# Expert weights two rows to a partition, gathers spread over two groups, results added later as a one-hot times two split parts

## The chip, the cores and the metric

The kernel runs on one core of a Trainium2 chip. The core has five engines that run side by side: TensorE (PE, matrix products; its weight loads are listed apart as PEld), VectorE (DVE), ScalarE (ACT), GpSimd (POOL) and SyncE (SP, which here only issues transfers). Sixteen DMA engines move data between the main memory and the core's on-chip memory. The metric is the time of one execution on the device, in microseconds (us); lower is better.

## The reference, cut to what matters

The program is four transformer layers on 256 tokens of width 1024, all in float32: two layers of a first block (each a mixer and a mixture of experts) and two dense layers of a second block. The change touches the mixture of experts:

```python
def expert_choice_ffn(h, w_router, w1, w3, w2):
    n_tok, d = h.shape[1], h.shape[2]
    cap = EC_FACTOR * n_tok // N_EXPERTS                  # 2 * 256 // 16 = 32
    aff = jax.nn.softmax(jnp.einsum('bnd,de->bne', h, w_router).astype(jnp.float32), axis=-1)
    gate, idx = lax.top_k(jnp.swapaxes(aff, 1, 2), cap)
    xs = jax.vmap(lambda hb, ib: hb[ib])(h, idx)
    a = jnp.einsum('becd,edf->becf', xs, w1)
    b = jnp.einsum('becd,edf->becf', xs, w3)
    y = jnp.einsum('becf,efd->becd', jax.nn.silu(a) * b, w2) * gate[..., None].astype(h.dtype)

    def combine(yb, ib):
        return jnp.zeros((n_tok, d), h.dtype).at[ib.reshape(-1)].add(yb.reshape(-1, d))
    return jax.vmap(combine)(y, idx)
```

Each of 16 experts picks 32 tokens, runs them through three 1024 x 1024 matrices (4 MB each) and the results are added back to the tokens with the gate as factor. In layer 0 this is done for two streams (256 latent and 256 context tokens) with the same weights, in layer 1 for the latent stream alone. So each layer reads 16 x 3 x 4 MB = 192 MB of expert weights, once.

## The kernel before, in words

`build` runs `even_mixer(0)`, `moe(0)`, `odd_mixer(1)`, `moe(1)` and `layers2`. All weights come through `wload`, which takes the next slot (a buffer of 128 partitions x 2048 float32, 1 MB) and issues one transfer on SP's queue. A slot can be filled again only when its last reader on PE is done, and SP issues in program order, so a slot that is still in use holds up all loads behind it. The slots come from `self.plan` while that list lasts, and then from `self.slots` in turn. In `moe(0)` `self.slots` has 13 entries; the plan adds two buffers that are needed later for scatter tables (`early`) and three that are needed later for gathered tokens (`spare`: the tiles xs3, xs2, xs1), so the first 18 loads find a buffer each, and from then on 13 are cycled. In `moe(1)` there are 16 slots, and 21 in the first pass.

`moe` makes the router's softmax and a top-32 of each expert, and from it one-hot matrices: `OH` (token x slot, for gathering) and `og` (the same with the gate as value). Experts run in four groups of four. `gather(g, ...)` multiplies the tokens (stationary operand, 128 columns at a time) by a group's columns of `OH`, which gives the tokens of four experts transposed (tile gps), and applies gain and shift on its way to `xs[g]`. `expert(e, ...)` takes each matrix in four loads of two row blocks (rows k*128 to k*128+127, so that partition p gets row p of each block: two runs of 4 KB); tokens are the stationary operand, the weights stream past. The hidden vector is transposed (hps) and multiplied by the third matrix (py), and the rows go to `y4` with the factor m5. After the first expert `scatter_rows` transposes `og` (tiles t, om) and broadcasts m5 (rb). `combine(g, ...)` multiplies the transposed `og` by the group's `y4` in float32 (tile cmb) and adds the product to the tokens.

In program order: gather of group 0 inside expert 0; gathers of groups 1, 2 and 3 behind experts 1, 2 and 3; a combine behind each of experts 3, 7, 11 and 15. The tile framework may start an instruction earlier on its engine where the operands are ready. The last combine carries hooks that start the next stage (`odd_start` or `block2_start`).

For comparison with other transfers: the modulation weights (`modulation`, in_mod_w) are also loaded by `wload`, with kk = 1 and n = 2048, that is one run of 8 KB per partition.

Of the kernel before, what the change touches and what calls it, by code (L numbers as in the profile page):

```python
# [80 lines left out]
class Net:  # L81
# [70 lines left out]

    def wload(self, src, kk, n):
        slot = self.plan.pop(0) if self.plan else None
        if slot is None:
            slot = self.slots[self.turn % len(self.slots)]
            self.turn += 1
        if type(slot) is tuple:
            pool, tag, bufs = slot
            t = pool.tile([P, 2048], F32, tag=tag, name="w", bufs=bufs)  # L160
        else:
            t = slot
        v = t[:, :kk * n].rearrange("p (k n) -> p k n", k=kk)
        self.nc.sync.dma_start(out=v, in_=src.rearrange("(k p) n -> p k n", p=P))
        return v
# [826 lines left out]
    def moe(self, L, streams):  # L992
        nc, A = self.nc, self.A
        ns = len(streams)
        T = 32 * ns
        HF = 128 // T
        CW = D // HF
        from contextlib import ExitStack
        with ExitStack() as st:
# [4 lines left out]
            n = self.extra[L]  # L1004
# [3 lines left out]
            act, wk = self.act, self.wk  # L1008
            ga = self.gain("norm2_g", L, 4)
            b3 = self.mod_cols(L, 3)  # L1010
            base = self.slots
# [14 lines left out]
            ps = self.tp.tile([P, 256], F32, tag="t", name="affT")  # L1026
# [47 lines left out]

            def room(i):
                return act.tile([P, 2048], F32, tag="om%d" % i, name="om%d" % i)
            early = [room(i) for i in range(ns)]

            def xs_tile(g):
                n = NK * 4 * T if g == 0 else 2048  # L1080
                xs = (rb[-1] if L == 0 and g > 1 else act).tile([P, n], F32, tag="xs%d" % g, name="xs%d" % g, bufs=1)
                return xs[:, :NK * 4 * T].rearrange("p (k e j) -> p k e j", k=NK, e=4)
# [21 lines left out]
            def expert(e, xs, y4, hooks={}):  # L1104
                pa = ab.tile([P, CW], F32, tag="ab", name="pa")
                pb = ab.tile([P, CW], F32, tag="ab", name="pb")
                for dst, nm in ((pa, "exp_w1"), (pb, "exp_w3")):
                    for k0 in range(0, NK, 2):
                        if (nm, k0) in hooks:
                            hooks[nm, k0]()  # L1110
                        w = self.wload(A[nm][L, e, k0 * P:(k0 + 2) * P, :], 2, D)
                        for kk in range(2):
                            for h in range(HF):
                                nc.tensor.matmul(dst[h * T:(h + 1) * T, :], xs[:, k0 + kk, e % 4, :],  # L1114
                                                 w[:, kk, h * CW:(h + 1) * CW], start=k0 + kk == 0,
                                                 stop=k0 + kk == NK - 1, skip_group_check=True)
# [5 lines left out]
                for j in range(nj):  # L1122
                    nc.tensor.transpose(ps[:, j, :], h[:, j * P:(j + 1) * P], self.ident)
                hT = wk.tile([P, 4, P], F32, tag="ht", name="ht")
                self.evac(hT[:, :nj, :], ps[:, :nj, :])
                py = yp.tile([P, CW], F32, tag="md", name="py")
                for k0 in range(0, NK, 2):
                    w = self.wload(A["exp_w2"][L, e, k0 * P:(k0 + 2) * P, :], 2, D)
                    for kk in range(2):
# [8 lines left out]
                if r == 0:  # L1138
                    y4 += [wk.tile([P, D], F32, tag="y4_%d" % s, name="y4") for s in range(ns)]
                for s in range(ns):  # L1140
# [4 lines left out]

            def combine(g, y4, hooks={}):
                i = 0
                for s, x in enumerate(streams):
                    for t in range(2):
                        for n in range(2):  # L1150
                            ps = self.mm.tile([P, 512], F32, tag="mm", name="cmb")
                            nc.tensor.matmul(ps, late["OT"][s][:, g, t * P:(t + 1) * P], y4[s][:, n * 512:(n + 1) * 512],  # L1152
                                             start=True, stop=True)
                            for f in hooks.get(i, ()):
                                f()
                            i += 1
                            xv = x[:, t, n * 512:(n + 1) * 512]
                            nc.vector.tensor_tensor(xv, xv, ps, op=ALU.add)
                for f in hooks.get(i, ()):
                    f()  # L1160

            xs = [xs_tile(0)]
            gather(0, xs[0], 2, [0])
            spare = [(rb[-1] if L == 0 and g > 1 else act).tile([P, 2048], F32, tag="xs%d" % g, name="wx", bufs=1)
                     for g in (3, 2, 1)]
            if L:
                spare.append(self.spare.rearrange("p t d -> p (t d)"))
            self.turn = 0
            self.plan = self.slots[:6] + early + self.slots[6:] + spare

            def scatter_rows():
                om = [room(i) for i in range(ns)]
                late["OT"] = OT = [om[s][:, :1024].rearrange("p (g n) -> p g n", g=4) for s in range(ns)]
                late["m5"] = m5 = [om[s][:, 1024:] for s in range(ns)]
# [6 lines left out]
            for g in range(4):  # L1181
                y4 = []
                for e in range(4):
                    expert(g * 4 + e, xs[g], y4, first if g == e == 0 else {})
                    if g == 0 and e:
                        xs.append(xs_tile(e))
                        gather(e, xs[e])
                if g == 2 and L:
                    self.fgb = self.spare[:, 0, :]
                    self.row_bcast(self.fgb, self.gcol["final_g"])  # L1190
                if g == 3:
                    self.slots = base
                    self.turn = 0
                combine(g, y4, {} if g < 3 else self.block2_start(streams[0]) if L else self.odd_start(streams[0]))

# [558 lines left out]
```

## Time and profile before

| what | value |
|---|---|
| median of 3 runs | 2343.78 us (2340.2 to 2344.97) |
| the profiled execution, its own time | 2342.45 us |
| its span in the trace | 2340.5 us |
| busy: PE, DVE, ACT, POOL | 2065.9, 967.8, 734.0, 206.8 us |
| moved by DMA | 634.09 MB in 205464 packets |
| bytes read from main memory | 631.02 MB |

How to read it: the profile records one execution; its own time is 1.95 us longer than its span. The span is cut into 40 slices of 58.5 us for the rows of busy tenths. PEclk is the share of full TensorE clock that was granted (1.00 is 2.4 GHz, 0.50 is 1.2 GHz). DMA is the mean busy share of the 16 DMA engines; it can be a little over 1 where packets overlap. A float32 product appears as two MATMUL instructions on PE.

### The profile page before, as it was taken

To read this page: it belongs to the slowest core of one execution; us is meant where nothing else is said; L and a number is where in the kernel's file an instruction comes from. 1 tells how busy PE (TensorE), PEld (TensorE's weight loads), DVE (VectorE), ACT (ScalarE), POOL (GpSimd) and SP (SyncE) were. 2 spreads that over 40 slices of the span, in tenths; PEclk is the share of its full clock that TensorE was granted. 3 is DMA by queue.
4 is the path that set the end of the run, shared out by engine and by line. 5 is a ranking of instruction groups with operands and counts; after the bars stand their busy time and mean duration, and the time that the engine had idled before them with its cause. 6 is when DMAs were issued, how large, how long until landed. Compare 5 with 4: busy or idle time off the path is not lost.

```text
span 2340.5 us, 31104 instructions
## 1 busy us (share of the span) xinstructions
PE 2065.9 (88%) x12723; PEld 1329.3 (57%) x12727; DVE 967.8 (41%) x1704; ACT 734.0 (31%) x1205; POOL 206.8 (9%) x254
## 2 busy tenths in 40 slices
PE   6999899988787799886665667999999999999998
PEld 3656644322222577542222224777799988778997
DVE  4456622221111656421010104456665565566555
ACT  4345211000000344210000002674554457655443
POOL 1001100000000110100000002111211102121112
PEclk8999999999999999897677867999999999999999
DMA  8547589999999666999999997434556553345562
GB/s 323 198 154 263 223 313 393 365 409 409 409 409 409 217 219 231 363 408 409 408 408 409 408 409 282 144 136 136 166 176 203 182 191 138 120 158 189 170 208 72
DMA packets 205464, 634.09 MB, mean 271 GB/s; under 512 B 12221, under 2 KB 16906, under 8 KB 199178
## 3 DMA queue, kind: packets, MB, share of 16 engines
q1 hardware_dynamic: 204074, 630.53, 71.6%
q8 instruction: 100, 1.64, 0.3%
q10 hardware_dynamic: 1248, 1.58, 0.2%
q14 instruction: 42, 0.34, 0.0%
HBM read 631.02 MB, written 1.05 MB: 270 GB/s over the span
## 4 chain that ended last, share of the span: by engine, by line
PE 67%; DMA 26%; DVE 4%; ACT 1%; issue 1%; POOL 1%; SPq 0%; DVEq 0%; ACTq 0%; POOLq 0%
DMA w<-in_exp_w_dram 25%; PE ps L237 8%; PE ps L239 8%; PE ps L238 8%; PE ups L1344 8%; PE acc L1344 7%; PE pa L1114 4%; PE pb L1114 3%; PE py L1133 3%; PE mod L403 2%; PE gps L1091 2%; PE S L541 2%; PE cmb L1152 1%; DMA w<-in_mod_w_dram 1%; PE Z L1344 1%
## 5 line engine op out<-in xcount | busy, mean ns | idle before, releaser
L177 DVE TENSOR_TENSOR wl<-w,wh 128x1024 fp32r<-128x1024 f32 (+2 forms) x333 | 410.4, 1253 | 167.1 <-ACT wh L176 158.8
L176 ACT CAST wh<-w 128x1024 fp32r<-128x1024 f32 (+2 forms) x337 | 338.1, 1026 | 172.5 <-PE acc L1344 69.6
L1114 PE MATMUL pb<-w,xs 128*32 128x256 f32 (+1 forms) x1440 | 208.0, 540 | 69.4 <-DMA w<-in_exp_w_dram 68.0
L1114 PE MATMUL pa<-w,xs 128*32 128x256 f32 (+1 forms) x1528 | 212.7, 522 | 49.7 <-DMA w<-in_exp_w_dram 48.3
L1133 PE MATMUL py<-w,ht 128*32 128x256 f32 (+1 forms) x1520 | 202.8, 527 | 55.2 <-DMA w<-in_exp_w_dram 40.2
L1119 DVE TENSOR_TENSOR sa<-sa,pb 128x512 f32<-128x512 f32 (+1 forms) x32 | 17.8, 555 | 455.8 <-PE pb L1114 429.4
L1118 ACT ACTIVATE sa<-pa 128x512 f32<-128x512 f32 (+1 forms) x32 | 15.7, 491 | 593.4 <-PE pa L1114 593.3
L237 PE MATMUL ps<-wh,hT 128*128 128x512 f32 x468 | 187.5, 401 | 2.1 <-ACT z L1295 1.7
L239 PE MATMUL ps<-wh,hT 128*128 128x512 f32 x468 | 183.5, 392 | 0.0
L238 PE MATMUL ps<-wl,hT 128*128 128x512 f32 x468 | 183.3, 392 | 0.0
L1114 PEld LDWEIGHTS pb<-w,xs 128*32 128x32 f32 (+1 forms) x1440 | 67.4, 136 | 201.0 <-DMA w<-in_exp_w_dram 99.4
L1143 DVE TENSOR_TENSOR y<-py,om 32x512 f32<-32x512 f32 (+1 forms) x128 | 70.9, 554 | 252.2 <-PE py L1133 249.3
L1114 PEld LDWEIGHTS pa<-w,xs 128*32 128x32 f32 (+1 forms) x1528 | 68.3, 132 | 178.7 <-DMA w<-in_exp_w_dram 79.5
L1133 PEld LDWEIGHTS py<-w,ht 128*32 128x32 f32 (+1 forms) x1520 | 67.9, 134 | 174.4 <-DMA w<-in_exp_w_dram 73.2
L1344 PE MATMUL acc<-wh,u 128*128 128x512 f32 x512 | 160.4, 390 | 0.0
L1344 PE MATMUL ups<-hh,wl 128*128 128x256 f32 x512 | 145.0, 283 | 0.0
L1344 PE MATMUL ups<-hh,wh 128*128 128x256 f32 x512 | 145.0, 283 | 0.0
L1344 PE MATMUL ups<-hl,wh 128*128 128x256 f32 x512 | 144.9, 283 | 0.0
L1344 PEld LDWEIGHTS acc<-wh,u 128*128 128x128 f32 x512 | 96.1, 188 | 19.7
L237 PEld LDWEIGHTS ps<-wh,hT 128*128 128x128 f32 x468 | 88.2, 188 | 23.8 <-ACT z L1295 2.1
L1344 PE MATMUL acc<-wl,u 128*128 128x512 f32 x256 | 99.8, 390 | 0.0
L239 PEld LDWEIGHTS ps<-wh,hT 128*128 128x128 f32 x468 | 88.3, 189 | 18.8
(439 smaller groups left out, 3273.4 us busy)
## 6 DMA issues: line engine op xcount, KB each, us to landing
w<-in_exp_w_dram SPq DMA_DIRECT2D x374, 1024.0 KB, 18.5
w<-in_w_in_dram SPq DMA_DIRECT2D x60, 1024.0 KB, 5.5
w<-in_mod_w_dram SPq DMA_DIRECT2D x48, 1024.0 KB, 7.1
w<-in_w_up_dram SPq DMA_DIRECT2D x32, 1024.0 KB, 5.5
w<-in_w_down_dram SPq DMA_DIRECT2D x32, 1024.0 KB, 5.0
w<-in_w_o_dram SPq DMA_DIRECT2D x8, 1024.0 KB
w<-in_ev_w_in_dram SPq DMA_DIRECT2D x7, 1024.0 KB
wx<-in_exp_w_dram SPq DMA_DIRECT2D x6, 1024.0 KB, 12.0
```

The source lines that it names most:

```text
L176: nc.scalar.copy(vh, raw)
L177: (eng or nc.vector).tensor_tensor(vl, raw, vh.bitcast(F32), op=ALU.subtract)
L237: nc.tensor.matmul(ps[:, :nb], a, wh[:, cols], start=j == 0, stop=False)
L238: nc.tensor.matmul(ps[:, :nb], a, wl[:, cols], start=False, stop=False)
L239: nc.tensor.matmul(ps[:, :nb], b, wh[:, cols], start=False, stop=j == kt - 1)
L403: nc.tensor.matmul(ps[32 * j:32 * j + 32, :], self.sc[:, k, :], w[:, 0, j * 512:(j + 1) * 512], start=k == 0, stop=k == NK - 1, skip_group ...
L541: nc.tensor.matmul(Sv[e][:, :nk], a[:, t * P:(t + 1) * P], b, start=i == 0, stop=masks is None and i == len(qk[e]) - 1, skip_group_check=True)
L1091: nc.tensor.matmul(ps[:, s * nj + j, :], streams[s][:, t, (k + j) * P:(k + j + 1) * P], OH[s, t][:, g * P:(g + 1) * P], start=t == 0, stop ...
L1114: nc.tensor.matmul(dst[h * T:(h + 1) * T, :], xs[:, k0 + kk, e % 4, :], w[:, kk, h * CW:(h + 1) * CW], start=k0 + kk == 0, stop=k0 + kk == ...
L1133: nc.tensor.matmul(py[n * T:(n + 1) * T, :], a, w[:, kk, n * CW:(n + 1) * CW], start=c == 0, stop=c == NK - 1, skip_group_check=True)
L1143: nc.vector.tensor_tensor(y4[s][r:r + 32, n * CW:(n + 1) * CW], py[p0:p0 + 32, :], late["m5"][s][r:r + 32, n * CW:(n + 1) * CW], op=ALU.mult)
L1344: nc.tensor.matmul(ps, a, b, start=start, stop=stop, skip_group_check=True)
```

## The change

1. `wload` gets `paired`: the expert weights are loaded so that partition p holds rows 2p and 2p+1 of a 256-row block, which are neighbours in memory (8 KB together). To match, token columns and hidden columns are taken with step 2 (`paired`), as stationary operands of the gather and of the transposes, and gains and shifts are permuted once per layer by eight small products (`paired_gains`).
2. The gathers of groups 1, 2 and 3 are cut into halves, which follow experts 1 and 2, 4 and 5, 6 and 7. The buffers xs3 and xs2 stay in the slot plan until then: for the second and third pass the plan has 15 slots (13 + 2), for the fourth 14, and then 13 (layer 0).
3. The transposed one-hot is stored as exact 0 and 1 in fp32r, and the gate as a column of its own (a maximum over the row). `parts_of` scales a group's rows by the gate and splits them into a high fp32r part (ACT) and the rest (DVE); `combine` multiplies the one-hot by both parts.
4. Groups 0 and 1 are combined inside expert 8, group 2 inside expert 12 (`combine_steps`), group 3 at the end.

```diff
-    def wload(self, src, kk, n):
+    def wload(self, src, kk, n, paired=False):
...
+        if type(slot) is list:
+            for k, t in enumerate(slot):
+                self.nc.sync.dma_start(out=t, in_=src.rearrange("(p k) n -> p k n", p=P)[:, k, :])
+            return slot
...
-        self.nc.sync.dma_start(out=v, in_=src.rearrange("(k p) n -> p k n", p=P))
+        self.nc.sync.dma_start(out=v, in_=src.rearrange("(p k) n -> p k n" if paired else "(k p) n -> p k n", p=P))
...
-            ga = self.gain("norm2_g", L, 4)
-            b3 = self.mod_cols(L, 3)
+            gb = act.tile([P, 2, NK, 2], F32, name="gb")
+            self.paired_gains(gb, L)
+            ga, b3 = gb[:, 0], gb[:, 1]
...
-                                nc.tensor.matmul(ps[:, s * nj + j, :], streams[s][:, t, (k + j) * P:(k + j + 1) * P],
+                                nc.tensor.matmul(ps[:, s * nj + j, :], self.paired(streams[s][:, t, :], k + j),
...
-                    nc.tensor.transpose(ps[:, j, :], h[:, j * P:(j + 1) * P], self.ident)
+                    nc.tensor.transpose(ps[:, j, :], self.paired(h, j), self.ident)
...
+            def parts_of(g, y4, s, ns):
+                ys = late["ys"]
+                for n in ns:
+                    yb = y4[s][:, n * 512:(n + 1) * 512]
...
+                    gt = late["gate"][:, s, 0, g:g + 1]
+                    nc.scalar.activation(yh, yb, AF.Copy, scale=gt)
+                    nc.vector.scalar_tensor_tensor(yl, yb, gt, yh.bitcast(F32), op0=ALU.mult, op1=ALU.subtract)
+                    late["y", n] = yh, yl
...
+                        for c in range(2):
+                            nc.tensor.matmul(ps, late["OT"][s][:, g, t * P:(t + 1) * P], late["y", n][c],
+                                             start=c == 0, stop=c == 1)
...
-            self.plan = self.slots[:6] + early + self.slots[6:] + spare
+            self.plan = self.slots[:6] + early + self.slots[6:] + spare + wide
+            for n in (2, 2, 1):
+                self.plan += self.slots + spare[:n]
...
-                        self.tr4(OT[s][:, :, t * P:(t + 1) * P], ogs[s, t])
...
+                        nc.vector.tensor_scalar(OT[s][:, :, t * P:(t + 1) * P], ps, 0.0, None, op0=ALU.is_gt)
+                        nc.vector.tensor_reduce(gate[:, s, t], ps, axis=AX.X, op=ALU.max)
...
+            turns = {1: (1, 0), 2: (1, 1), 4: (2, 0), 5: (2, 1), 6: (3, 0), 7: (3, 1)}
...
+                if e == 8:
+                    hooks = dict(zip(places, combine_steps([(0, rows[0]), (1, rows[1])], 1)))
+                if e == 12:
+                    hooks = dict(zip(places, combine_steps([(2, rows[2])], 2)))
...
+    def paired(x, k):
+        c = k // 2 * 2 * P + k % 2
+        return x[:, c:c + 2 * P - 1:2]
```

## Rows read from the trace of the kernel before

**Rows 1.** The page: span, busy tenths in 40 slices, DMA packets.

```profile
span 2340.5 us, 31104 instructions
...
DMA  8547589999999666999999997434556553345562
GB/s 323 198 154 263 223 313 393 365 409 409 409 409 409 217 219 231 363 408 409 408 408 409 408 409 282 144 136 136 166 176 203 182 191 138 120 158 189 170 208 72
DMA packets 205464, 634.09 MB, mean 271 GB/s; under 512 B 12221, under 2 KB 16906, under 8 KB 199178
```

**Rows 2.** Windows of both expert stages; the last three columns: PEclk, DMA share, GB/s.

```profile
296.00:308.00 12.00, 12.00 (x70) 7.07 (x70) 1.46 (x4) 3.50 (x6) 0.00 (x0) 1.00 0.78 278
308.00:360.00 52.00, 51.92 (x278) 23.95 (x276) 13.25 (x23) 6.76 (x14) 0.00 (x0) 1.00 0.89 338
360.00:416.00 56.00, 56.00 (x309) 27.81 (x306) 14.10 (x28) 8.24 (x19) 0.00 (x0) 1.00 1.03 410
416.00:428.00 12.00, 12.00 (x40) 3.97 (x42) 4.81 (x7) 0.00 (x0) 0.00 (x0) 1.00 0.51 194
500.00:760.00 260.00, 210.11 (x876) 61.29 (x873) 42.47 (x62) 7.12 (x12) 0.00 (x0) 1.00 1.03 409
964.00:1424.00 460.00, 312.29 (x3272) 130.48 (x3272) 62.28 (x150) 19.86 (x46) 3.38 (x4) 0.76 1.03 409
```

**Rows 3.** PE's order of time, layer 0: gathers, first combine, an undisturbed expert.

```profile
347.14 1.16 PE L1091 MATMUL gps<-OH,xl 128*128 128x128 f32 x8
...
353.89 6.65 PE L1114 MATMUL pa<-w,xs 128*64 128x512 f32 x29
...
383.96 6.65 PE L1114 MATMUL pa<-w,xs 128*64 128x512 f32 x29
...
415.89 6.84 PE L1152 MATMUL cmb<-y,om 128*128 128x512 f32 x14
...
444.90 7.04 PE L1114 MATMUL pa<-w,xs 128*64 128x512 f32 x32
...
468.02 7.04 PE L1114 MATMUL pa<-w,xs 128*64 128x512 f32 x32
```

**Rows 4.** SP's order of time: modulation loads, expert loads of both layers.

```profile
2.37 2.06 SPq L164 DMA_DIRECT2D w<-in_mod_w_dram  x4
...
277.83 0.73 SPq L164 DMA_DIRECT2D wx<-in_exp_w_dram  x1
294.52 186.24 SPq L164 DMA_DIRECT2D w<-in_exp_w_dram  x70
...
920.12 30.05 SPq L164 DMA_DIRECT2D w<-in_exp_w_dram  x11
```

**Rows 5.** Windows: modulation loads (8 KB runs), then a short burst of expert loads.

```profile
8.00:16.00 8.00, 6.57 (x37) 3.08 (x40) 4.28 (x18) 2.51 (x4) 0.00 (x0) 1.00 1.01 423
44.00:48.00 4.00, 4.00 (x19) 3.06 (x17) 2.19 (x12) 1.06 (x3) 1.62 (x4) 1.00 1.01 428
932.00:936.00 4.00, 4.00 (x26) 3.45 (x26) 3.16 (x13) 0.59 (x1) 0.00 (x0) 1.00 1.03 423
```

**Rows 6.** Groups by line and form, 290 to 780 us (layer 0).

```profile
L1152 PE MATMUL cmb<-y,om 128*128 128x512 f32 x64 | 31.2, 618 | 3.2 <-DVE y L1143 2.4 <-DVE xl L1158 0.9
L1091 PEld LDWEIGHTS gps<-OH,xc 128*128 128x128 f32 x120 | 14.7, 192 | 0.8 <-issue 0.8
L1119 DVE TENSOR_TENSOR sa<-sa,pb 128x512 f32<-128x512 f32 x16 | 11.0, 689 | 220.5 <-PE pb L1114 194.1 <-issue 26.4
L1118 ACT ACTIVATE sa<-pa 128x512 f32<-128x512 f32 x16 | 9.6, 597 | 280.1 <-PE pa L1114 280.1
```

**Rows 7.** PE's order of time: end of layer 1 and the products behind it.

```profile
1428.07 5.92 PE L1152 MATMUL cmb<-y,om 128*128 128x512 f32 x8 [0.95 <-DVE y L1143]
...
1443.16 0.40 PE L238 MATMUL ps<-eb,hT 128*128 128x512 f32 x1
1443.39 0.39 PE L239 MATMUL ps<-eb,hT 128*128 128x512 f32 x1
```

More of the change, by code (lines that the diff above doesn't have):

```diff
@@ L1073, in moe, with room, xs_tile @@
             late = {}
[L1075 to L1076 removed]
+            def room(i, dts=(F32, F32)):
+                return [act.tile([P, D], dt, tag="om%d%d" % (i, j), name="om") for j, dt in enumerate(dts)]
             early = [room(i) for i in range(ns)]
[L1079 removed]
+            def xs_tile(g, dt=F32, shaped=True):
                 n = NK * 4 * T if g == 0 else 2048
[L1081 to L1082 removed]
+                xs = (rb[-1] if L == 0 and g > 1 else act).tile([P, n], dt, tag="xs%d" % g, name="xs%d" % g, bufs=1)
+                return xs if dt == F32R or not shaped else xs[:, :NK * 4 * T].rearrange("p (k e j) -> p k e j", k=NK, e=4)
             def gather(g, xs, nj=4 // ns, ks=None):
@@ L1138, in expert @@
                 if r == 0:
-                    y4 += [wk.tile([P, D], F32, tag="y4_%d" % s, name="y4") for s in range(ns)]
+                    if e == 4:
+                        ys = xs_tile(0, F32, False)
+                        y4 += [ys[:, s * D:(s + 1) * D] for s in range(ns)]
+                    else:
+                        y4 += [wk.tile([P, D], F32, tag="y4_%d" % s, name="y4") for s in range(ns)]
                 for s in range(ns):
@@ L1144, in expert @@
                                                 late["m5"][s][r:r + 32, n * CW:(n + 1) * CW], op=ALU.mult)
[L1146 to L1159, printed above, removed]
-                    f()
+            def parts_of(g, y4, s, ns):
+                ys = late["ys"]
+                for n in ns:
+                    yb = y4[s][:, n * 512:(n + 1) * 512]
+                    i = n % (ys.shape[1] // 1024)
+                    yh, yl = [ys[:, (2 * i + c) * 512:(2 * i + c + 1) * 512] for c in range(2)]
+                    gt = late["gate"][:, s, 0, g:g + 1]
+                    nc.scalar.activation(yh, yb, AF.Copy, scale=gt)
+                    nc.vector.scalar_tensor_tensor(yl, yb, gt, yh.bitcast(F32), op0=ALU.mult, op1=ALU.subtract)
+                    late["y", n] = yh, yl
@@ new lines, in combine @@
+            def combine(g, s, ns, hooks={}):
+                x = streams[s]
+                for t in range(2):
+                    for n in ns:
+                        ps = self.mm.tile([P, 512], F32, tag="mm", name="cmb")
+                        for c in range(2):
+                            nc.tensor.matmul(ps, late["OT"][s][:, g, t * P:(t + 1) * P], late["y", n][c],
+                                             start=c == 0, stop=c == 1)
+                        for f in hooks.get(2 * t + n, ()):
+                            f()
+                        xv = x[:, t, n * 512:(n + 1) * 512]
+                        nc.vector.tensor_tensor(xv, xv, ps, op=ALU.add)
+                for f in hooks.get(4, ()):
+                    f()
@@ new lines, in combine_steps, with step @@
+            def combine_steps(todo, home):
+                todo = [(g, y4, s) for g, y4 in todo for s in range(ns)]
+                for i, (g, y4, s) in enumerate(todo):
+                    def step(i=i, g=g, y4=y4, s=s):
+                        if not i:
+                            late["ys"] = xs_tile(home, F32R)
+                            parts_of(g, y4, s, (0, 1))
+                        combine(g, s, (0, 1))
+                        if i + 1 < len(todo):
+                            parts_of(*todo[i + 1], (0, 1))
+                    yield step
@@ L1180, in moe @@
             first["last"] = scatter_rows
[L1181 to L1188, printed above, removed]
+            nj = 4 // ns
+            halves = [[0, 2], [4, 6]] if L == 0 else [[0], [4]]
+            turns = {1: (1, 0), 2: (1, 1), 4: (2, 0), 5: (2, 1), 6: (3, 0), 7: (3, 1)}
@@ new lines, in moe @@
+            places = [(nm, k) for nm in ("exp_w1", "exp_w3") for k in range(2, NK, 2)]
+            rows = {}
+            for e in range(16):
+                g = e // 4
+                hooks = first if e == 0 else {}
+                if e == 8:
+                    hooks = dict(zip(places, combine_steps([(0, rows[0]), (1, rows[1])], 1)))
+                if e == 12:
+                    hooks = dict(zip(places, combine_steps([(2, rows[2])], 2)))
+                expert(e, xs[g], rows.setdefault(g, []), hooks)
+                if e in turns:
+                    to, half = turns[e]
+                    if not half:
+                        xs.append(xs_tile(to))
+                    gather(to, xs[to], nj, halves[half])
+                if e == 11 and L:
@@ L1189, in moe @@
                     self.fgb = self.spare[:, 0, :]
                     self.row_bcast(self.fgb, self.gcol["final_g"])
[L1191 to L1194, printed above, removed]
+            self.slots = base
+            self.turn = 0
+            hooks = self.block2_start(streams[0]) if L else self.odd_start(streams[0])
+            late["ys"] = xs_tile(3, F32R)
@@ new lines, in moe, with paired_gains @@
+            for s in range(ns):
+                parts_of(3, rows[3], s, (0, 1))
+                combine(3, s, (0, 1), {} if s else hooks)
+    @staticmethod
+    def paired(x, k):
+        c = k // 2 * 2 * P + k % 2
+        return x[:, c:c + 2 * P - 1:2]
+    def paired_gains(self, out, L):
+        nc = self.nc
+        ga = self.gain("norm2_g", L, 4)
+        for i, src in enumerate((ga, self.mod_cols(L, 3))):
+            st = src.rearrange("p (a h) s -> p h a s", h=2)
+            ps = self.tp.tile([P, 2, NK // 2, 2], F32, tag="t", name="pgp")
+            for b in range(2):
+                for h in range(2):
+                    nc.tensor.matmul(ps[h * 64:h * 64 + 64, b], self.ident[:, b:P:2], st[:, h], start=b == 0,
+                                     stop=b == 1, skip_group_check=True)
+            nc.vector.tensor_copy(out[:, i].rearrange("p (a b) s -> p b a s", b=2), ps)
```

24 lines of the change are left out of this document (14 added, 10 removed).

## The prediction

> **What bounds the kernel now.** I read the slices of the page first. Of the 40, two stretches of eight to nine slices show about 409 GB/s with the DMA engines full [rows 1]: these are the two mixture-of-experts stages, and at the same time PE is not the full engine there. The windows say it sharper. From 500 to 760 us (layer 0) and from 964 to 1424 us (layer 1) the DMA share is 1.03 at 409 GB/s throughout, while PE is busy 210 of 260 us and 312 of 460 us [rows 2]. So these stages last as long as their loads: 1 MB (1.0486e6 bytes) at 409 GB/s is 2.56 us, 12 of them (one expert) 30.8 us. PE needs less: an undisturbed expert of layer 0 is 23.1 us from one pa to the next (444.90 to 468.02), and with a gather behind it 30.1 us (353.89 to 383.96) [rows 3], so a gather costs 7.0 us of PE time.
>
> The start of layer 0 is different. There PE is full (clock 1.00) and the DMA is not: 278 GB/s from 296 to 308, 338 from 308 to 360, 194 from 416 to 428 [rows 2]. The reader is to see two kinds of time: where DMA is full, only a faster transfer helps; where PE is full and DMA has gaps, the gaps come from slots that PE has not yet released. In us of full transfer the gaps are 12 x (1-278/409) = 3.8, 52 x (1-338/409) = 9.0 and 12 x (1-194/409) = 6.3, together 19.1. The last one sits exactly under the first combine (cmb, 14 of its 16 instructions, from 415.89) [rows 3], when PE reads no weights for over 8 us. The first 18 loads had been issued by 278; load 19 waits until 294.52, when PE has used the first slot [rows 4].
>
> **Part 1, longer runs.** A load of two rows per partition has one 8 KB run where it had two of 4 KB; three of the 384 loads go into split buffers and keep 4 KB. The trace has 8 KB runs: the modulation loads (205464-199178 = 6286 packets are not under 8 KB [rows 1], and 48 such loads of 128 make 6144). While four of them queue [rows 4], 8 to 16 us moves 423 GB/s, and 44 to 48 us 428 [rows 5]. Against 409 that is 3.3 to 4.4%. But these are short: expert loads in 4 KB runs also reach 423 in 4 us when only a few are in flight [rows 4, 5], and settle to 409 in the long stream. So the long-stream rate of 8 KB runs is not shown. Lower bound 409 (the limit is in bytes, no gain), upper bound 428. I take 421: if what slows the long stream is paid per run, it is paid half as often, and the loss from 428 is half of that from 423 to 409, which is 7.
>
> Stretch bound by DMA: 360 to 764 in layer 0 less the gap that is counted apart (404-12 = 392 us), and 460 us in layer 1 [rows 2]. At 421 each us becomes 409/421: 392 x 0.0285 = 11.2 and 460 x 0.0285 = 13.1, sum 24.3. Bounds: 0 at 409, and at 428 852 x 0.0444 = 37.8.
>
> The Trainium skill weighs in twice here. "DMA: Bandwidth & Descriptors", section Bandwidth, part "Why small descriptors are slow", has a fixed cost of about 3 cycles per packet beside one cycle per 32 bytes; by that 4 KB costs 131 cycles and two of them 262 against 259, a gain of 1.2%, and the part would give 852 x 0.012 = 10 instead of 24.3. The trace has more than that between its 409 and its 423 to 428. Its table "Measured" in the same section has 425 GB/s for one long transfer of 16 MB, which is on the side of 421 rather than 409; no run here shows such a transfer.
>
> **Part 2, gathers and combine moved away from the start.** Until expert 4, PE loses two of three gathers and the combine: 2 x 7.0 + 8.6 = 22.6 us less work between 347 and 423, and what is left comes in halves of 3.5 us. PE then runs 23.1 to 26.6 us per expert against 30 of the DMA, so it falls behind nowhere, and the gap at 416 (6.3) goes wholly. Of the 9.0 before 360, the part behind the pauses of scatter and first gather shrinks, since from load 32 on a load waits for the slot of 15 loads ago and no longer of 13, which is 5 us more of transfer in reserve; the part inside expert 0 stays, as does the 3.8. I take 6.7 of the 12.8, sum 13.0; bounds 6.3 and 19.1.
>
> Where do the moved pieces go? Two gathers (14 us) to experts 4 to 7, combine of groups 0 and 1 to expert 8, of group 2 to expert 12. An expert has 30.8-23.1 = 7.7 us of slack on PE (at 421 GB/s 29.9-23.1 = 6.8), and PE may lag by up to 13 loads (32 us) before a transfer waits. Half gathers of 3.5 fit. Expert 8 takes four steps, each eight fp32r products of 512 columns (0.23 us from start to start at full clock [rows 7]: 1.9 us) and four DVE additions at 0.69 (the nearest row of that shape [rows 6]: 2.8 us) plus the splits (two DVE at 0.69, two ACT at 0.60 [rows 6]); some 3 to 4 us a step, up to 16 us in one expert, less than two experts' slack. Hidden; if the lag were already full, it would cost those 16 us. In layer 1 PE is busy two thirds of the time [rows 2], all of this is hidden.
>
> **Part 3, what is added on the path.** Scatter: four tiles that DVE and ACT emptied in turn now need two DVE instructions each (8 x 0.69 = 5.5 us in a stretch of 6 to 7 us): +1 in layer 0, between 0 and 4. Gains by eight small products per layer, before the router has ended: PE idles there; +0.5 in each layer, between 0 and 2. Last combine: its rows must be scaled and split before the first product: ACT 0.60 + DVE 0.69 = 1.3 us per stream. In return a block of 512 columns takes two fp32r products (0.47 us) instead of a float32 one (31.2/64 = 0.49 an instruction, of two [rows 6]). In layer 0, where DVE additions set the pace, +1. In layer 1 the clock is low at that point and the eight instructions take 5.92 us [rows 7], 0.74 each, so the cheaper product gives back what the split costs: 0. Bounds for both ends together -2 and +4.
>
> Stationary operands with step 2 (gather, hidden transposes) have no row before. The nearest is the unit-step weight load, 192 ns, of which PE shows little [rows 6]. I take 0; the upper bound is a second 192 ns for each, a rival below.
>
> **Sum.** 2342.45 - 24.3 - 13.0 + 1 + 1 + 1 = 2308.2 for an execution like the profiled one. It lies 1.3 below the median of the runs shown, so for a median 2309; I say 2308.
>
> **Rivals.**
> - *The long stream has a byte limit.* Then part 1 gives 0, and 2342.45 - 13 + 3 = 2332. For it: 4 KB runs also start at 423 and fall to 409 [rows 5, 2], so the fall may not care for run length. Against it: exactly the packets are what the change halves. It also covers that a transfer is still carried out in 4 KB pieces. The Trainium skill ("DMA: Bandwidth & Descriptors", Specifications) asks for at least 512 B for line rate; by that rule 4 KB has nothing left to gain, and the time is this rival's.
> - *Slower: strided weight loads make PE the bound in layer 0.* Layer 0 has four gathers of 64 instructions and 16 transposes of 4, 320 instructions. PE's work from 292 is about 28 + 7 (expert 0, scatter) + 15 x 23.1 + 21 + 18 (gathers, steps) = 420 us; the loads need 174 x 2.49 = 433. Above 13 us of extra PE work each us costs one. If a step-2 load takes twice 192 ns and the second half shows, that is 320 x 0.19 = 61 us: 48 lost, against 24.3 + 13 won with part 1's layer-1 share untouched: 2308 + 48 = 2356. It decides the sign from about 0.14 us per instruction. Against it: PEld is busy 61 of 260 us [rows 2], much of a load can lie under products.
> - *The early gaps stay.* Scatter's pause or order of slots keeps DMA waiting as before: 2342.45 - 24.3 + 3 = 2321. Against it: the gap at 416 lies under an instruction that goes away [rows 2, 3].
>
> **How the numbers follow.** My forecast (both parts, 415 to 428 GB/s) 0.64, with its own range 2295 to 2320. Byte limit 0.18, at 2325 to 2337. Early gaps stay 0.08, about 2321. Strided loads 0.10, 2335 to 2375, mostly slower. The range from 2295 to 2333 takes in the first, the third and most of the second. About 0.2% (4.7 us) is what a measurement of this kernel can tell from no change. Faster 0.88, same 0.04, slower 0.08.
>
> **What would show it.** Packets of 8 KB or more rise from 6286 to some 50000 and the total falls by as many. Windows in the long streams show 415 to 428 GB/s; if they show 409, step 1 failed. The first pause of DMA at about 416 is gone and the rate from 360 on has no gap until the last load. Layer 1's stage is shorter by about 13 us, layer 0's by about 21. The weight loads of gps keep their 192 ns; if they double, the slower rival is at work. The prediction is wrong if a wait appears in the loads behind an xs buffer on SP, or if combine steps in expert 8 open a DMA gap at that place.

## The result and the profile after

| | before | after |
|---|---|---|
| median | 2343.47 us (2340.2 to 2344.97, 4 runs) | 2309.65 us (2307.15 to 2310.7, 4 runs) |
| span of the profiled execution | 2340.5 us | 2308.6 us |

The ratio is 0.9856, with a 95% interval of 0.9839 to 0.9873: the changed kernel is faster by 33.8 us, and the forecast of 2308 lies 1.7 us beside the median. Timed once more, it had 2308.05 us against 2342.7 (ratio 0.9849, 0.9836 to 0.9862).

The page of the changed kernel, in the lines that answer to [rows 1]:

```profile
span 2308.6 us, 31250 instructions
...
DMA  8547589999999476999999996435555544355552
GB/s 327 201 154 257 220 332 421 418 418 421 422 421 398 157 258 244 354 420 421 420 421 421 421 421 235 147 104 162 174 186 179 201 164 142 124 171 177 183 199 74
DMA packets 156746, 634.10 MB, mean 275 GB/s; under 512 B 12270, under 2 KB 16955, under 8 KB 101691
```

The bytes are the same, the packets are 48718 fewer, and those of 8 KB or more rose from 6286 to 156746-101691 = 55055. Where the full slices had 408 or 409 GB/s they have 418 to 422.

The windows that answer to [rows 2], of the same columns:

```profile
296.00:308.00 12.00, 12.00 (x70) 6.87 (x68) 1.46 (x4) 2.97 (x6) 0.00 (x0) 1.00 0.80 270
308.00:360.00 52.00, 51.92 (x262) 21.86 (x260) 15.49 (x27) 5.08 (x10) 0.00 (x0) 1.00 0.97 397
360.00:416.00 56.00, 56.00 (x298) 26.19 (x296) 11.96 (x23) 6.61 (x15) 0.00 (x0) 1.00 1.01 421
416.00:428.00 12.00, 10.74 (x58) 5.30 (x54) 0.69 (x1) 0.32 (x1) 0.00 (x0) 1.00 1.01 421
500.00:740.00 240.00, 206.24 (x876) 66.38 (x876) 55.10 (x82) 15.45 (x24) 0.00 (x0) 0.99 1.01 421
980.00:1380.00 400.00, 269.54 (x2862) 112.87 (x2858) 50.03 (x108) 17.72 (x40) 0.00 (x0) 0.77 1.01 420
```

Two things are to be seen. The long streams are at 420 to 421. And the gap at 416 (194 before) is gone, while 308 to 360 went from 338 to 397; only the first 12 us stayed (278, now 270). From 320 to 430 us the rate is 421, so that what is left lies ahead of 320. The gaps that are left are 12 x (1-270/421) + 52 x (1-397/421) = 7.3 us, where [rows 2] gave 19.1.

PE's order of time, with the instructions that answer to [rows 3]: the pa groups of experts 2 and 3 with a half gather between them, and of two experts with none in between.

```profile
350.66 7.09 PE L1121 MATMUL pa<-w,xs 128*64 128x512 f32 x32
...
376.19 7.09 PE L1121 MATMUL pa<-w,xs 128*64 128x512 f32 x32
...
463.32 7.04 PE L1121 MATMUL pa<-w,xs 128*64 128x512 f32 x32
...
486.47 7.04 PE L1121 MATMUL pa<-w,xs 128*64 128x512 f32 x32
```

With half a gather an expert takes 25.5 us of PE, with none 23.15; both are less than the 12 x 2.49 = 29.9 us that its loads take. So from 320 us on PE no longer holds the loads up.

**Where the time went.** PE's order of time has four marks that every run of this study shows: the first pa of layer 0, the end of the last py of layer 0, the first rsb behind it (the odd stage's scatter product, which needs the finished tokens), and the first gps of layer 1. They cut the span into five parts that add up to it:

```
us                         to first pa  layer 0, first pa   tail, last py  rsb to     first gps  span
                                        to end of last py   to rsb         first gps  to end
before                     292.49       473.82              17.87          190.23     1366.09    2340.5
changed                    293.23       449.59              21.06          190.95     1353.77    2308.6
changed, second time       295.89       449.63              20.00          189.36     1351.02    2305.9
pairing alone              295.48       467.51              17.89          192.01     1351.81    2324.7
order alone                292.34       460.89              21.07          192.88     1364.12    2331.3
gathers early              296.07       460.55              20.81          189.50     1351.37    2318.3
combines early             293.30       458.42              21.06          188.59     1354.03    2315.4
last group whole           295.64       449.93              17.88          189.74     1351.61    2304.8
last group whole, again    292.47       449.91              17.88          189.48     1352.36    2302.1
13 slots                   294.96       453.45              20.62          189.57     1352.10    2310.7
```

The first part varies by about 3 us between executions of the same kernel (293.23 and 295.89), and the shift is there before anything of the change runs: the last product of layer 0's router (lgt) starts at 274.41 and 277.54 us. The fourth part varies by 1.6 and the fifth by 2.8. The second and third are steady within 0.1 and 1.1 us for the same kernel; so these two parts tell more than the whole time. Of the 31.9 us between the two profiled executions, layer 0's loads give 24.2, the tail takes 3.2 back, the stretch from layer 1's first gather to the end gives 12.3, and the first and fourth parts, in which the change has the eight small products of each layer, take 0.7 each. What those products cost is hidden there under the variation; it is read behind, under the gains.

### The profile page after: what moved, and what is told of

The parts are those of the page before. It is cut to its first block, busy times and chain, and to the rows that moved or that the text cites. A ratio compares the mean times of both kernels' runs of the same rounds, so it can differ in the third digit from the quotient of the medians.

```text
span 2308.6 us, 31250 instructions
## 1 busy us (share of the span) xinstructions
PE 2054.4 (89%) x12759; PEld 1340.9 (58%) x12759; DVE 987.7 (43%) x1744; ACT 747.9 (32%) x1226; POOL 206.3 (9%) x254
## 2 busy tenths in 40 slices
DMA packets 156746, 634.10 MB, mean 275 GB/s; under 512 B 12270, under 2 KB 16955, under 8 KB 101691
## 4 chain that ended last, share of the span: by engine, by line
PE 65%; DMA 26%; DVE 5%; issue 2%; ACT 1%; POOL 1%; SPq 0%; DVEq 0%; ACTq 0%; POOLq 0%
DMA w<-in_exp_w_dram 25%; PE ps L242 8%; PE ps L244 8%; PE ps L243 8%; PE ups L1419 8%; PE acc L1419 7%; PE py L1140 3%; PE pa L1121 3%; PE pb L1121 3%; PE mod L408 2%; PE gps L1097 2%; PE S L546 2%; PE Z L1419 1%; DMA w<-in_mod_w_dram 1%; PE S L1419 1%
## 5 line engine op out<-in xcount | busy, mean ns | idle before, releaser
L1154 DVE TENSOR_TENSOR y<-py,om 32x512 f32<-32x512 f32 (+1 forms) x96 | 53.2, 554 | 174.8 <-PE py L1140 172.9
## 6 DMA issues: line engine op xcount, KB each, us to landing
w<-in_exp_w_dram SPq DMA_DIRECT2D x380, 1024.0 KB, 19.8
```

The source lines that it names most:

```text
L1154: nc.vector.tensor_tensor(y4[s][r:r + 32, n * CW:(n + 1) * CW], py[p0:p0 + 32, :], late["m5"][s][r:r + 32, n * CW:(n + 1) * CW], op=ALU.mult)
```

## The experiments

The kernel before, timed beside them, had 2342.99 us (beside pairing alone, order alone, gathers and combines early), 2342.3 (13 slots, last group whole) and 2342.7 (the last two).

### Pairing alone

The kernel before, with only the two rows per partition (and the step-2 columns and permuted gains that they need):

```diff
...
-                        w = self.wload(A[nm][L, e, k0 * P:(k0 + 2) * P, :], 2, D)
+                        w = self.wload(A[nm][L, e, k0 * P:(k0 + 2) * P, :], 2, D, True)
...
-                    nc.tensor.transpose(ps[:, j, :], h[:, j * P:(j + 1) * P], self.ident)
+                    nc.tensor.transpose(ps[:, j, :], self.paired(h, j), self.ident)
...
```

> The kernel before with the paired loads alone (and the step-2 columns and permuted gains that they need); gathers, slots and combine as before. My theory: the long streams run at 421 GB/s instead of 409, which gives 24 us where the loads are the limit, less some 2 us where PE sets the pace from 360 to 416 us (30.1 us per expert): 2320 to 2323 us. The gap of the transfers under the first combine stays. Rival (the gain of the change came from the order and only little from the runs): 2332 or more. The rate in the long stretches should be 420 to 422 GB/s.

Measured: 2323.38 us (2322.08 to 2327.59), ratio 0.9921 (0.9909 to 0.9934), 0.4 us above the expected range; the long streams run at 421 and 420. Layer 1 took its whole share (1366.09 to 1351.81), layer 0 only 6.3 us. Its windows of the start of layer 0 say why:

```profile
332.00:344.00 12.00, 12.00 (x64) 5.36 (x62) 1.75 (x4) 0.60 (x1) 0.00 (x0) 1.00 0.85 335
...
356.00:368.00 12.00, 12.00 (x65) 5.03 (x65) 0.73 (x2) 1.65 (x4) 0.00 (x0) 1.00 0.76 289
...
416.00:428.00 12.00, 12.00 (x42) 4.89 (x42) 6.55 (x12) 1.73 (x5) 0.00 (x0) 1.00 0.54 223
428.00:440.00 12.00, 12.00 (x56) 3.86 (x52) 0.01 (x1) 0.60 (x1) 0.00 (x0) 1.00 0.88 334
440.00:452.00 12.00, 10.43 (x49) 3.77 (x50) 2.89 (x5) 0.58 (x1) 0.00 (x0) 1.00 1.01 425
```

PE is full (11.92 of 12 us or more) in every window from 296 to 440 us: with the old order it paces most of the stage until there, and faster loads only wait longer for its slots. The gap at 416 even gets a second part (428 to 440). Counted in windows of 12 us over the 192 us behind the first pa, in us of full transfer (409 or 421), the gaps add up to 22.6 in the kernel before and to 27.8 here.

### Order alone

The changed kernel with the weights in 4 KB runs again, unit-step columns and unpermuted gains:

```diff
...
-        self.nc.sync.dma_start(out=v, in_=src.rearrange("(p k) n -> p k n" if paired else "(k p) n -> p k n", p=P))
+        self.nc.sync.dma_start(out=v, in_=src.rearrange("(k p) n -> p k n", p=P))
...
-        c = k // 2 * 2 * P + k % 2
-        return x[:, c:c + 2 * P - 1:2]
+        return x[:, k * P:(k + 1) * P]
```

> The changed kernel with the expert weights loaded as before (rows k*128 to k*128+127, two runs of 4 KB per partition, columns in steps of one): gathers, slots and combine as in the changed kernel. My theory: 409 GB/s in the long streams, the gaps at the start of layer 0 gone as in the changed kernel: 10 to 13 us won against the kernel before, 2330 to 2334 us. Rival (the order alone does as much as both together): 2315 or less.

Measured: 2331.44 us (2330.46 to 2333.35), ratio 0.9949 (0.9936 to 0.9963). Layer 0's loads are 12.9 us shorter (counted as above, its gaps add up to 9.6 us, 13.0 fewer), its tail is 3.2 us longer, and its stream stays at 409 (500 to 740 us). Layer 1 and behind moves by 2 us only, which is within the variation. In layer 0's loads pairing gives 6.3 alone and the order 12.9 alone, 19.2 in sum, and both together 24.2: the new order is what lets the faster loads count at the start.

### Gathers early

The changed kernel with whole gathers of groups 1, 2 and 3 behind experts 1, 2 and 3 again; the buffers xs2 and xs3 are then needed at once, so the later passes of the plan have 13 slots.

```diff
-            for n in (2, 2, 1):
-                self.plan += self.slots + spare[:n]
...
-                if e in turns:
-                    to, half = turns[e]
-                    if not half:
-                        xs.append(xs_tile(to))
-                    gather(to, xs[to], nj, halves[half])
+                if e in (1, 2, 3):
+                    xs.append(xs_tile(e))
+                    gather(e, xs[e], nj)
```

> The changed kernel with the gathers of groups 1, 2 and 3 whole behind experts 1, 2 and 3 and without the extra passes of the slot plan (13 slots from load 32 on), as before; combine stays late. My theory: PE works 30 us per expert there against 29.9 of the loads, so the transfers get gaps of 3 to 7 us between 320 and 420 us: 2313 to 2317 us against 2309.7 of the changed kernel. Rival (only the combine's place matters): 2309 to 2311.

Measured: 2319.94 us (2319.02 to 2321.41), ratio 0.9902 (0.9888 to 0.9915): 10 us over the changed kernel, 3 to 7 more than expected. It all lies in layer 0's loads (460.55 against 449.6). The windows have new gaps at 332 and 356 us:

```profile
332.00:344.00 12.00, 12.00 (x64) 5.32 (x61) 2.93 (x6) 1.18 (x2) 0.00 (x0) 1.00 0.78 309
344.00:356.00 12.00, 12.00 (x71) 6.53 (x69) 4.96 (x11) 1.61 (x4) 0.00 (x0) 1.00 0.98 360
356.00:368.00 12.00, 12.00 (x64) 5.21 (x64) 0.96 (x3) 2.21 (x5) 0.00 (x0) 1.00 0.76 281
```

### Thirteen slots

To separate the two halves of that edit, the changed kernel with its half gathers but without the buffers of xs2 and xs3 in the later passes (the two lines about the plan above, nothing else).

> The changed kernel without the buffers of xs3 and xs2 in the later passes: from load 32 on 13 slots are cycled, as in the kernel before. Everything else as changed. Theory (the early gather of whole groups is what the third experiment paid for, the two extra slots little): 2310 to 2314. Rival (reserve is what counts, as the prediction had it with up to 6.7 us for gaps ahead of 360 us): 2315 to 2320, and layer 0's last load lands 6 to 10 us later.

Measured: 2312.47 us (2311.64 to 2313.82), ratio 0.987 (0.9857 to 0.9883). Layer 0's loads take 453.45 us: 3.8 more for two slots less, and then 460.55-453.45 = 7.1 more for the early whole gathers. So both halves count, the gathers about two parts of three.

### Combines early

The changed kernel with each group combined right behind its last expert, in two split parts as before. The combine adds to the tokens in place, so that groups 2 and 3, which are gathered behind experts 4 to 7, get tokens that already carry group 0's result; this run computes something else there.

```diff
...
-                if e == 8:
-                    hooks = dict(zip(places, combine_steps([(0, rows[0]), (1, rows[1])], 1)))
-                if e == 12:
-                    hooks = dict(zip(places, combine_steps([(2, rows[2])], 2)))
...
+                if e in (3, 7, 11):
+                    late["ys"] = xs_tile(g, F32R)
+                    for s in range(ns):
+                        for cs in ((0, 1),) if late["ys"].shape[1] == 2048 else ((0,), (1,)):
+                            parts_of(g, rows[g], s, cs)
+                            combine(g, s, cs)
```

> The changed kernel with each group combined right behind its last expert (still as one-hot times two parts); gathers and slots as in the changed kernel. By the step of the prediction the gap of the transfers under the first combine returns, 6 us: 2314 to 2317 us. Rival: with the gathers moved PE is no longer late when the combine comes, the loads in reserve cover it, and the time is that of the changed kernel, 2308 to 2311.

Measured: 2316.99 us (2314.51 to 2317.61), ratio 0.9887 (0.9873 to 0.99). Layer 0's loads take 8.8 us more than in the changed kernel. The gap is back, later and longer:

```profile
428.00:440.00 12.00, 12.00 (x70) 6.51 (x70) 1.89 (x5) 2.20 (x5) 0.00 (x0) 1.00 0.89 330
440.00:452.00 12.00, 11.99 (x68) 5.90 (x66) 4.11 (x8) 1.51 (x4) 0.00 (x0) 1.00 0.94 335
452.00:464.00 12.00, 11.15 (x60) 4.95 (x56) 2.15 (x5) 2.21 (x5) 0.00 (x0) 1.00 0.92 334
464.00:476.00 12.00, 11.22 (x46) 3.60 (x46) 2.87 (x5) 0.00 (x0) 0.00 (x0) 0.86 0.93 339
```

In GB/s of 421 that is 12 x (4 - (330+335+334+339)/421) = 9.9 us, about the loss. With the gathers spread over two groups the combines must stand behind experts 7 and later anyway; the run shows that this is also the cheaper place. It moves the combines and puts each in one piece, where the changed kernel has steps between the loads of an expert; the two aren't told apart.

### The loads by themselves

Nothing but transfers: the expert weights in seven stages of one run length each, with nothing that reads them (the list has KB per run, buffers, number of loads); the output is raw weights, and the time (683 us) stands beside nothing.

```diff
...
+STAGES = [(4, 10, 40), (8, 10, 40), (2, 10, 40), (16, 5, 20), (32, 3, 10), (4, 3, 30), (8, 3, 30)]
...
```

> Only the transfers are left: expert weights are loaded in seven stages one after the other, with nothing that reads them, and the output is raw weights; the time stands beside nothing. Stages: runs of 4, 8 and 2 KB (1 MB loads, ten buffers), 16 KB (2 MB loads, five), 32 KB (4 MB loads, three), then again 4 and 8 KB with only three buffers of 1 MB. Theory (a cost per run): the 409 GB/s of 4 KB runs and the 421 of 8 KB runs give 9 ns per run and 151 ns per 4 KB on each of the 16 engines; so 2 KB runs should stream at about 387, 16 KB at 427, 32 KB at 430, and the 4 and 8 KB stages repeat 409 and 421 without any work on the engines. Rival (the difference between 409 and 421 comes from something else in the kernel, such as when slots come free): both stages show the same rate, and 2 KB too. The stages with three buffers tell whether few loads in flight, not run length, give the 423 to 428 of short stretches: then both rise by some 1 to 3 per cent; if not, they show 409 and 421 or less.

Measured, in windows from inside each stage in the order of the list (columns: window, its length, POOL busy, PEclk, DMA share, GB/s):

```profile
60.00:80.00 20.00, 0.00 (x0) 1.00 1.03 410
...
160.00:180.00 20.00, 0.00 (x0) 1.00 1.01 422
...
240.00:260.00 20.00, 0.00 (x0) 1.00 1.05 387
...
360.00:380.00 20.00, 0.00 (x0) 1.00 1.00 428
...
460.00:480.00 20.00, 0.00 (x0) 1.00 1.01 434
...
560.00:580.00 20.00, 0.00 (x0) 1.00 1.03 410
...
640.00:660.00 20.00, 0.00 (x0) 1.00 1.01 422
```

2 KB runs stream at 387, 4 KB at 410, 8 KB at 422, 16 KB at 428, 32 KB at 434 (431 in the window behind it): within 1% of a fixed 9 ns per run beside 151 ns per 4 KB on each engine. The engines do nothing here, so the difference between 409 and 421 belongs to the transfers. With three buffers the rates are the same 410 and 422: few loads in flight don't make a stream faster. (The stages of 16 and 32 KB also have larger loads and fewer buffers, and the 2 KB runs are half rows with a gap between them in memory. The whole was run once.)

### The last group not split

The changed kernel, but in layer 0 POOL multiplies the gate into m5 behind expert 11, and the last group's combine takes the exact one-hot times the float32 rows:

```diff
...
+                if e == 11 and L == 0:
+                    for s in range(ns):
+                        nc.gpsimd.tensor_scalar(late["m5"][s], late["m5"][s], late["gate"][:, s, 0, 3:4], None, op0=ALU.mult)
...
-                parts_of(3, rows[3], s, (0, 1))
-                combine(3, s, (0, 1), {} if s else hooks)
+                if not whole:
+                    parts_of(3, rows[3], s, (0, 1))
+                combine(3, s, (0, 1), {} if s else hooks, rows[3][s] if whole else None)
...
```

> The changed kernel, but in layer 0 the last group is not split: the gate is multiplied into m5 on POOL behind expert 11, and the last combine multiplies the one-hot by the float32 rows, so no split stands in layer 0's tail. Theory (the tail of layer 0 is some 3 us longer than before because two splits per stream stand on DVE ahead of its additions and of what follows): 3 us less, 2306 to 2308, and the time from the last landing to the odd stage's scatter falls from 23.0 to about 20 us. Rival (the tail is longer for another reason, such as the order of the odd stage's own work): no change, 2308 to 2311.

Measured: 2306.56 us (2306.02 to 2307.81), ratio 0.9845 (0.9831 to 0.9858). DVE's order of time in the tail, first of the changed kernel:

```profile
742.86 2.83 DVE L1154 TENSOR_TENSOR y<-py,om 32x512 f32<-32x512 f32 x4 [7.68 <-PE py L1140]
745.73 1.42 DVE L1166 SCALAR_TENSOR_TENSOR xs<-y,sl,xs 128x512 fp32r<-128x512 f32 x2
747.37 1.35 DVE L1181 TENSOR_TENSOR xl<-xl,cmb 128x512 f32<-128x512 f32 x2 [0.22 <-PE cmb L1176]
...
750.83 1.41 DVE L1166 SCALAR_TENSOR_TENSOR xs<-y,sl,xs 128x512 fp32r<-128x512 f32 x2
752.45 0.69 DVE L1181 TENSOR_TENSOR xc<-xc,cmb 128x512 f32<-128x512 f32 x1 [0.22 <-PE cmb L1176]
```

and then of the one whose last group is whole:

```profile
745.62 2.83 DVE L1154 TENSOR_TENSOR y<-py,om 32x512 f32<-32x512 f32 x4 [8.89 <-PE py L1140]
748.49 1.29 DVE L1184 TENSOR_TENSOR xl<-xl,cmb 128x512 f32<-128x512 f32 x2
...
752.30 0.69 DVE L1184 TENSOR_TENSOR xc<-xc,cmb 128x512 f32<-128x512 f32 x1 [0.36 <-PE cmb L1176]
```

From the start of the last y rows to the first addition it is 747.37-742.86 = 4.5 us with the splits and 748.49-745.62 = 2.9 without, and the second pair of splits takes another 1.4 between the streams. The tail falls from 21.06 to 17.88 us, what it was before the change.

Because the two had not been timed beside each other, and their intervals overlap, both were run again side by side, the changed kernel first:

> The changed kernel once more, on the same chip and beside the kernel whose last group in layer 0 is not split, because the two had been timed beside different runs of the kernel before and their intervals overlap. Expected as before: 2308 to 2311.

> The kernel whose last group in layer 0 is not split, beside the changed kernel. Theory (the splits cost the tail 3 us): 2.5 to 3.5 us less than the changed kernel in the same call, 2305 to 2308, and from the end of the last product of expert 15 to the odd stage's first scatter product 17.9 us instead of 21.1. Rival (the first result of 2306.6 was one chip's luck): less than 1 us apart.

Measured: 2308.05 us (2306.73 to 2310.87) and 2307.18 us (2304.02 to 2311.1), ratios 0.9849 (0.9836 to 0.9862) and 0.9847 (0.9834 to 0.9861). The tails were 20.0 and 17.88 us. So the tail is shorter each time, by 2.1 to 3.2 us, but the whole time doesn't show it: 0.9 us apart, as the rival had it, where 2.5 to 3.5 were expected, and single runs of one kernel lie 4 to 7 us apart. The place is shown; a gain in the time is not.

## Why the prediction was right

The two large terms came out by the mechanism that the prediction gave for them, each shown by a run of its own. That the total lies within 1.7 us of the median owes something to luck. The terms as measured below are 24.2 us of layer 0's loads and 10.9 of layer 1's, less 2.0 and 1.1 for the gains and 3.2 for the last combine: 28.8 us (31.0 the second time), where the sum had 34.3. The other 3.1 (3.6) us between the executions lie in stretches for which the sum has no term or a term of 0, ahead of layer 0's router, in the odd stage and behind layer 1's loads.

**Longer runs (step 1).** Right in value and in cause. It took 421 between 409 and 428; the trace has 420 to 421, and the transfers by themselves 422 against 410. The byte-limit rival falls with that. The 423 to 428 of short stretches [rows 5], which the prediction used as its upper end, are not the long-stream rate of 8 KB runs, and three buffers don't bring them about; what does was not settled. The fixed cost in the Trainium skill ("DMA: Bandwidth & Descriptors", section Bandwidth, "Why small descriptors are slow") gave an estimated 1.2% for this step; the runs show 422/410, 2.9%. By the Specifications of the same page of the Trainium skill, 512 B is enough for line rate; the streams of 2 to 32 KB, from 387 to 434 GB/s, disagree.

**Start of layer 0 (step 2).** Right: the gap at 416 went, and of the 19.1 us of gaps 11.8 were won where 13.0 were taken. The two experiments that put gathers or combines back bring gaps back, and cost 8.8 to 11 us of layer 0's loads. Under the first combine PE reads no weights for the 6.84 us of its row [rows 3], not for over 8, which changes nothing in the sum. Steps 1 and 2 together were 11.2 + 13.0 = 24.2 us of layer 0, and it got 24.2 shorter; that the two are equal is chance, since the gaps gave 1.2 less than taken and the scatter (+1 in the sum) stands in the same stretch and wasn't told apart. But the text added them as if each stood alone. They don't: pairing alone wins only 6.3 of layer 0, because PE paces that stretch until the order is changed. For this change the sum holds, for one half of it it would not have.

**Moved pieces (step 2).** Hidden, as said: 500 to 740 us, with all the steps of the first combines in it, has no gap. A small one stands ahead of them, at 452 to 456 and 460 to 464 us (389 and 354), 0.9 us (1.7 the second time). With 13 slots throughout it isn't there (452 to 464: 423), so it comes with the extra passes of the slot plan. That it is the wait behind an xs buffer, which the prediction named as a sign of being wrong, is likely but not shown; its size decides nothing.

**Gains (step 3).** Mis-sized, and hidden in the whole time. The eight small products of each layer were put at +0.5, on the ground that PE idles there. In layer 0 it is 16.78 us from the last product of the router (lgt) to the first pa in the kernel before and 16.79 with the order alone; with the pairing it is 18.82 (18.35 the second time), and 18.81 to 18.83 in the six other runs that have it. So they cost 2.0 us (1.6), the upper bound. The first gather and what follows it up to the pa take 6.8 us either way; all of it is lost ahead of the gather. PE idles there, but DVE has work: its copy of the first result (gb, 275.19) comes after a wait of 1.19 us for PE, ahead of the router's own instructions on DVE. In layer 1, the kernel before and then the changed one:

```profile
964.31 0.40 PE L521 MATMUL lgt<-c,lgp 128*128 128x16 f32 x2 [0.36 <-ACT lgp L519]
...
974.41 2.93 PE L1091 MATMUL gps<-OH,xl 128*128 128x128 f32 x12 [1.01 <-DVE OH L1065]
```

```profile
943.67 0.39 PE L526 MATMUL lgt<-c,lgp 128*128 128x16 f32 x2 [0.36 <-ACT lgp L524]
943.99 0.41 PE L1267 MATMUL pgp<-gain,ident 128*64 128x8 f32 x8
...
954.83 2.93 PE L1097 MATMUL gps<-OH,xl 128*128 128x128 f32 x12 [1.01 <-DVE OH L1071]
```

That is 10.10 us and 11.16 (11.44 the second time): 1.1 to 1.3 us. Together the gains take about 3 us where 1 was put.

**Last combine (step 3).** The other term that was mis-sized. In layer 0 it was put at +1 and measured +3.2 (+2.1 the second time). The working had one pair of a split at 1.3 us per stream and took most of it as given back by cheaper products. But the products were not what the tail waited for: DVE's additions and the y rows before them were, and two DVE splits of 0.71 us per stream went onto that engine, the second stream's ahead of the additions of that stream.

**Layer 1.** Put at -13.1 for the stream, and mis-sized by some 2 us. From the first gps to the start of the last py it went from 451.0 to 440.1 us, 10.9 (439.2, or 11.8, the second time). The windows at its start show a loss:

```profile
956.00:960.00 4.00, 4.00 (x27) 2.51 (x26) 1.26 (x3) 0.46 (x1) 2.33 (x4) 0.50 1.01 424
960.00:964.00 4.00, 4.00 (x46) 2.87 (x49) 0.82 (x2) 0.91 (x2) 0.00 (x0) 0.98 0.97 328
964.00:968.00 4.00, 4.00 (x67) 2.26 (x63) 0.41 (x1) 1.64 (x2) 0.00 (x0) 1.00 0.93 346
968.00:972.00 4.00, 4.00 (x63) 2.36 (x59) 1.76 (x4) 0.49 (x2) 0.00 (x0) 1.00 0.99 375
```

4 x (3 - (328+346+375)/421) = 2.0 us are lost right behind the first gather (954.83), where the kernel before had 400 or more. The 21 slots of the first pass fill 21 x (2.56-2.49) = 1.5 us sooner, and PE's first release comes no earlier; that reading fits in size and place. Pairing alone loses 1.5 us at the same place (976 to 988 us: 354, 403 and 348), the order alone 0.4 (972 to 984: 400, 380 and 402), so the loss comes mostly with the faster loads. But pairing alone still has 13.2 us less from the first gps to the last py (437.8), so the loss alone doesn't explain the 2 us, and the rest stays open. From the first gps to the end of the span it is 12.3 to 15.1 us less; 1.1 to 2.5 of that lie behind the last cmb and weren't followed.

The end of layer 1, answering to [rows 7]:

```profile
1394.94 1.07 PE L1140 MATMUL py<-w,ht 128*32 128x256 f32 x16 [0.88 <-DMA w<-in_exp_w_dram]
1397.74 3.72 PE L1176 MATMUL cmb<-xs,om 128*128 128x512 f32 x6 [1.73 <-ACT xs L1165]
...
1401.98 1.22 PE L1176 MATMUL cmb<-xs,om 128*128 128x512 f32 x2
```

The first product now waits 1.73 us for the split, and the eight instructions run faster in return: from the start of the last py to the end of the last cmb it is 8.3 us, and it was 8.6. Here the 0 of the prediction holds.

**Slower rival.** Strided stationary operands cost little. The weight loads of the changed kernel's layer 0 (290 to 780 us):

```profile
L1097 PEld LDWEIGHTS gps<-OH,xc 128*128 128x128 f32 x120 | 15.9, 196 | 5.7 <-issue 5.7
...
L1130 PEld LDWEIGHTS hps<-ident,sa 128*128 128x128 f32 x64 | 8.9, 206 | 20.1 <-DVE sa L1126 20.1
```

The gather's went from 192 ns [rows 6] to 196, those on the latent stream (xl) from 191 to 203, and with the pairing alone to 205 and 207: 4 to 16 ns, far from the 0.14 us per instruction at which that rival decided the sign. The early gaps of the third rival went too.

## What to carry to other kernels

Where a stage shows full DMA, look at the length of the runs even if they are already 4 KB: halving their number was worth 2.9% of the rate of the long streams here. A faster transfer counts only where the transfers set the pace; cut first what the other engine does in the stretches with gaps, and cost the two edits together. What is added to the end of a stage is costed on the engine that the end waits for, and instruction by instruction, not on the one whose work got cheaper. The same holds for small work put into a chain of waits: the eight products went to an idle PE, and it was DVE, waiting for them, that was late.

## What was not expected of the hardware

A transposing product's weight load with step 2 (hps) took 206 ns where it had 141 with unit step, 46% more; its products went from 284 to 301 ns. It goes with the step and not with the order: pairing alone has 207 ns, the order alone 141. The gather's weight loads took only 2 to 8% more (192 and 191 ns before; 196 to 207).

The changed kernel's list of DMA issues (count, size, median us to landing) and its chain of waits (start, us) in layer 1:

```profile
w<-in_exp_w_dram SPq DMA_DIRECT2D x380, 1024.0 KB, 19.8
```

```profile
1133.57 19.84 DMA w<-in_exp_w_dram
1153.47 19.79 DMA w<-in_exp_w_dram
1173.32 19.83 DMA w<-in_exp_w_dram
```

A load lands 19.8 us after its issue, and the chain goes through the stage in such pieces. 19.8/2.49 is eight loads on the way at a time, though layer 1 has 16 to 21 slots; what sets the eight wasn't tried.
